# Transposed copies of x and memory from the host, one weight chunk for both token halves in the first block, and products on zeros during the first loads

## The chip, the cores and the metric

The kernel runs on 1 core of one Trainium2 chip. The metric is the device time of one execution in microseconds (us). Before the change it is 1037.3 us, the median of 3 runs (1035.68, 1037.3 and 1037.99 us).

The engines are named as in the profile: PE is TensorE (PEld its weight loads, which overlap with the products), ACT is ScalarE, DVE is VectorE, POOL is GpSimd, and SP is SyncE, whose queue issues all DMAs of this kernel.

## The reference

Two decoder layers work on 256 tokens of width 1024, beside 256 tokens of memory. Cut to what matters here:

```python
def rms_norm(x, gain):
    xf = x.astype(jnp.float32)
    y = xf * lax.rsqrt(jnp.mean(xf * xf, axis=-1, keepdims=True) + RMS_EPS)
    return (y * gain.astype(jnp.float32)).astype(x.dtype)

def swiglu(h, w_gate, w_up, w_down):
    return (jax.nn.silu(h @ w_gate) * (h @ w_up)) @ w_down

def memory_cross_attention(q_mem, mem_n, w_mem_kv, q_gain, k_gain):
    ...
    kv = mem_n @ w_mem_kv
    k = rms_norm(kv[..., :MEM_WIDTH].reshape(B, M, MEM_HEADS, HEAD_DIM), k_gain)
    v = kv[..., MEM_WIDTH:].reshape(B, M, MEM_HEADS, HEAD_DIM)
    ...
```

Layer 0 is x + 1/2 swiglu(norm(x)), then an mLSTM mixer beside attention to the memory, then a second half swiglu. Then keys and values for layer 1 are projected once. Layer 1 has a half swiglu, a dilated attention beside attention to the memory, and a last half swiglu. The hidden width of the swiglu is 2816. Each layer has its own gain for the memory (mem_norm) and its own w_mem_kv.

## The kernel before, in words

**Tiling.** The 256 tokens are two halves of 128 (t = 0 and 1). x stays on the chip as two [128, 1024] float32 tiles. A product contracts over the partitions, so x is needed transposed: `norm` (line 617) and `transposed` (line 590) turn 128x128 pieces of x on PE with an identity (into PSUM tile `tps`), ACT writes them times the gain as float32r (`xh`), and DVE writes what float32r leaves over (`xl`). The factor 1/rms of a token is applied later, where a product leaves PSUM.

**Three products for one.** Each weight chunk is split in the same way: ACT copies it to float32r (`hi`), DVE takes the difference (`lo`), and `mm3` (line 555) multiplies xh by lo, xh by hi and xl by hi into one PSUM bank.

**The weight stream.** `_stream` (line 48) lists all weights in the order of use as units of up to [128, 1024]. `load_unit` (line 462) issues the DMA of a unit into one of 6 tiles `raw`; `emit_unit` (line 473) splits it into one of 8 places `hi`, `lo`. A tile `raw` is free for the next load once DVE has taken `lo`; a place is free once the products of both halves have read it. In the first block (256 gate and 256 up columns of layer 0) a unit is one chunk of 128 rows, [128, 512], so 8 units; later a unit of a swiglu holds two chunks, [128, 1024].

**Order of the work.** The program is written out in one order by Python code that keeps rough cost tables of the engines (class `_Model`, line 168): PE's main stream is fixed, and side chains (splits, norms, activations) are put in where the tables say they are ready. Every engine, and SP's queue, then works strictly in the order in which its instructions were emitted.

**The swiglu.** `ffn` (line 720) runs 11 blocks of 256 hidden columns. `gu` makes a block for one half of the tokens: 8 chunks, three products each, 24 in all, into `gups`. `hidden` follows: silu on ACT (`sil`), the product with the up half on DVE (`h`), two transposes on PE (`tph`), the split to `hh` and `hl`. `dn` multiplies by w_down into four accumulators `acc`. In the first block, `gu(0, 0)` goes through all 8 units for half 0, and `gu(0, 1)` goes through them again for half 1.

**The memory.** `memory_load` (line 669) loads `mem` as two [128, 1024] tiles `mt`, once for each layer, and for layer 0 computes 1/rms. `memory_unit` (line 680) turns each tile on PE in two groups of four transposes and splits it into a place of the stream's ring, as the left operand of the products with w_mem_kv (`memory_kv`, line 787, PSUM tile `mkvps`).

**The start.** `run` (line 1341) loads the two halves of x[0], the identity, the gains, 5 weight units and x[1] in an order of its own, and puts the norms of both halves beside the main stream.

Of the kernel before, what the change touches and what calls it, by code (L numbers as in the profile page):

```python
# [35 lines left out]
FIRST = 4  # L36
TAIL = 3
START = 0.0
# [9 lines left out]
def _stream():  # L48
    """The weights in the order in which they are used: (key, source, slices, width)."""
# [37 lines left out]
    def memory(layer):  # L87
        units.append((("memT", layer, 0), None, 0))
        units.append((("memT", layer, 1), None, 0))
        single(("mkv", layer), "w_mem_kv", layer, 0, 512, 2)  # L90
# [23 lines left out]
def _pack(units, w):  # L114
    """Lay the weights out as one flat array, unit after unit, [128, width] each."""
    parts = []
    for _, src, _ in units:
        if src is None:
            continue
# [22 lines left out]
def _consts():  # L142
    """Constants of the shapes alone: identity, triangle, ones, selectors, T5 buckets, masks."""
# [122 lines left out]
class _Engine:  # L266
    """An engine of the core whose instructions the model follows."""
# [57 lines left out]
class _Chain:  # L325
    """A chain of steps that is emitted beside the main stream, each when the one before is done."""
# [6 lines left out]
class _Kernel:  # L333
# [74 lines left out]
    def until(self, t):  # L408
        """run the chains that are ready before the main stream can go on at t"""
# [19 lines left out]
    def wait(self, *chains):  # L429
        """in a chain: until others are done"""  # L430
# [30 lines left out]

    def load_unit(self):
        i, self.loaded = self.loaded, self.loaded + 1
        _, src, width = self.units[i]
        if src is None:
            return
# [6 lines left out]
    def emit_unit(self):  # L473
        """the next unit's steps begin: hi, the weights in float32r, and lo, what that leaves"""
        i, self.next = self.next, self.next + 1
        key, src, width = self.units[i]
# [11 lines left out]
        if src is None:  # L488
            c = self.spawn(self.memory_unit(key[2], hi, lo))
        else:  # L490
            while self.loaded <= i:
                self.room()
                self.load_unit()
            c = self.spawn(steps(self.raw.pop(i)))
            self.running.append(c)
            self.step(c)
# [11 lines left out]
    def unit_ready(self):  # L508
        """when the split of the next unit can begin without delaying other work"""
# [3 lines left out]
        if self.units[i][1] is None:  # L513
            return 0.0
# [19 lines left out]
    def release(self, *key):  # L534
        i = self.index[key]
        self.used[i] += 1
        while self.freed < len(self.units) and \
                self.used[self.freed] == (2 if self.units[self.freed][1] else 1):
# [27 lines left out]

    def rpow(self, ss, n, scale):
        """(ss * scale + eps) ** -0.5, [128, n]"""
# [7 lines left out]
    def rms(self, src, out, later=LATER):  # L576
        """out [128, 1] = 1 / rms of each row of src [128, 1024]"""
# [12 lines left out]
    def transposed(self, src, hi, lo, chunks, gain=None):  # L590
        """hi, lo [128, 8, 128] take the transposed 128-column chunks of src, times the gain"""
# [46 lines left out]
    def head_norm(self, src, n, out, rstd):  # L638
        """out = src * rstd normed over groups of 64; src [128, n*64] in PSUM"""
# [29 lines left out]
    def memory_load(self, layer):  # L669
        """the memory, ahead of its use"""  # L670
        self.mem_gain = self.gains[7 + layer]
        self.mem_tiles = []
        for m in range(2):
            mt = self.work.tile([P, D], F32, tag="mem", name="mt")
            self.nc.sync.dma_start(mt, self.io["mem"][0, m * P:(m + 1) * P, :])
            self.mem_tiles.append(mt)
            if layer == 0:
                self.mem_stats[m] = self.spawn(self.rms(mt, self.mem_rstd[m]))

    def memory_unit(self, m, hi, lo):  # L680
        mt = self.mem_tiles[m]
        yield from self.when(mt)
        h3, l3 = (a.rearrange("p (k t) -> p k t", k=NK) for a in (hi, lo))
        for h in range(2):
            yield from self.transposed(mt, h3, l3, [4 * h + j for j in range(4)], self.mem_gain)
            if h == 0:
                yield
# [16 lines left out]
    def block(self, x, key, n, kper, after):  # L704
        """a block of n columns of a projection; after(ps) are the steps that take it on"""
# [13 lines left out]

    def ffn(self, layer, which, after):  # L720
        nc = self.nc
        acc = [[self.acc.tile([P, 512], F32, tag="acc", name=f"acc{t}{h}") for h in range(2)]
               for t in range(2)]
        chains, hT = {}, {}
# [25 lines left out]
        def dn(b, t):  # L750
            self.finish(chains.pop((b, t)))
# [19 lines left out]
        for b in range(NB - 1):  # L771
            for t in range(2):
# [95 lines left out]
    def out_part(self, key, t, acc, haT, order, chunks, after=None):  # L868
        """some chunks of an output projection; the last ones end with the residual"""
# [21 lines left out]

    def mixer_a(self, after):
        nc, io = self.nc, self.io
        with ExitStack() as ctx:
# [44 lines left out]
            def gates():  # L939
                # u = i - cumsum(log sigmoid f), cg = max(0, running max of u)  # L940
# [165 lines left out]
            def first_block(t):  # L1106
                query_chains.append(self.block(t, ("a", "gq"), 264, 3, query(t)))
                if t == 1:
                    self.memory_load(0)
# [41 lines left out]

    def shared_kv(self, again):
# [49 lines left out]
        for b in range(3):  # L1202
            if b == 1:
                self.memory_load(1)
# [135 lines left out]

    def run(self, stop=None):
# [6 lines left out]
        nc.gpsimd.memset(self.mhalf, -0.5)  # L1348
# [102 lines left out]
```

## Time and profile before

| what | value |
|---|---|
| median of 3 runs | 1037.3 us (1035.68 to 1037.99) |
| span of the profiled execution | 1036.0 us |
| PE busy | 1019.0 us, 98% of the span, 4888 products and transposes |
| DVE busy | 616.1 us, 59% |
| ACT busy | 557.5 us, 54% |
| bytes moved by DMA | 182.53 MB, mean 176 GB/s |

The span runs from the first instruction to the last. Of the profiled execution the page gives the span alone, 1036.0 us; what lies around it is not told, and the 3 timed runs lie between 0.3 us below and 2.0 us above it.

To read it: the ends of products are modelled, so a product's own duration (0.39 us for 512 columns) is longer than its pitch, the time from the start of one to the start of the next (0.23 us). [...] A wait shows as a number in brackets behind a row: the idle time before it, and what ended it.

### The profile page before, as it was taken

What the parts mean: (1) busy time and instruction counts of PE and PEld (TensorE: products, weight loads), DVE (VectorE), ACT (ScalarE), POOL (GpSimd) and SP (SyncE); (2) the same over time, 40 slices, a digit from 0 to 9 for tenths busy, and PEclk for the clock granted to TensorE, in tenths of its full rate; (3) what the DMA queues carried; (4) which work ended last, traced back from release to release, by engine and by line L of the source; (5) the groups of instructions that cost most, each with busy time, mean ns of one, the idle gap of its engine ahead of it and who ended that gap; (6) DMA issues with size and microseconds to landing.
All of it is one profiled execution on the core that took longest, in us unless ns stands there. A gap on an engine that the chain in (4) does not pass through costs nothing.

```text
span 1036.0 us, 13199 instructions
## 1 busy us (share of the span) xinstructions
PE 1019.0 (98%) x4888; PEld 840.4 (81%) x4888; DVE 616.1 (59%) x903; ACT 557.5 (54%) x913; POOL 43.7 (4%) x78
## 2 busy tenths in 40 slices
PE   7999999999999999999999999999999999999998
PEld 5888888898888888888877888888887688888886
DVE  6655554767866755554565755455476865545452
ACT  7544453596775744454466644445366774545441
POOL 0000000111110000000011000000003000000000
PEclk9999999999999999999999999999999999999999
DMA  8764644553537465656454656464552246555531
GB/s 292 246 212 166 214 166 152 169 196 103 185 104 241 146 215 169 209 166 211 164 188 163 208 199 207 167 214 166 181 198 68 82 167 218 170 198 184 182 121 41
DMA packets 54329, 182.53 MB, mean 176 GB/s; under 512 B 6332, under 2 KB 8180, under 8 KB 54264
## 3 DMA queue, kind: packets, MB, share of 16 engines
q1 hardware_dynamic: 54264, 181.69, 52.0%
q8 instruction: 38, 0.62, 0.2%
q14 instruction: 27, 0.22, 0.1%
HBM read 180.60 MB, written 1.07 MB: 175 GB/s over the span
## 4 chain that ended last, share of the span: by engine, by line
PE 92%; DVE 3%; ACT 2%; DMA 1%; issue 1%; POOL 0%; SPq 0%; DVEq 0%; ACTq 0%
PE gups L545 47%; PE acc L545 23%; PE aps L545 6%; PE oacc L545 3%; PE bqps L545 2%; PE mkvps L545 2%; PE kvps L545 2%; PE tph L552 2%; PE tps L552 2%; DVE lo L276 1%; DMA raw<-in_wts 1%; PE sc L545 1%; DVE s L276 1%; PE ms L545 1%; PE po L545 0%
## 5 line engine op out<-in xcount | busy, mean ns | idle before, releaser
L276 DVE TENSOR_TENSOR lo<-raw,hi 128x1024 fp32r<-128x1024 f32 (+3 forms) x347 | 404.1, 1184 | 152.0 <-ACT hi L276 137.2
L276 ACT CAST hi<-raw 128x1024 fp32r<-128x1024 f32 (+3 forms) x347 | 349.3, 1021 | 110.7 <-PE acc L545 66.0
L545 PE MATMUL gups<-lo,xh 128*128 128x512 f32 x704 | 280.9, 399 | 1.3 <-DVE lo L276 1.3
L545 PE MATMUL gups<-hi,xl 128*128 128x512 f32 x704 | 275.8, 392 | 0.0
L545 PE MATMUL gups<-hi,xh 128*128 128x512 f32 x704 | 275.1, 391 | 0.0
L545 PEld LDWEIGHTS gups<-hi,xl 128*128 128x128 f32 x704 | 132.6, 188 | 28.5
L545 PEld LDWEIGHTS gups<-lo,xh 128*128 128x128 f32 x704 | 132.6, 188 | 28.5 <-DVE lo L276 2.9
L545 PEld LDWEIGHTS gups<-hi,xh 128*128 128x128 f32 x704 | 133.0, 189 | 25.9
L545 PE MATMUL acc<-lo,hh 128*128 128x512 f32 x352 | 141.8, 403 | 0.0
L545 PE MATMUL acc<-hi,hl 128*128 128x512 f32 x352 | 138.0, 392 | 0.0
L276 ACT ACTIVATE sil<-gups,rstd 128x256 f32<-128x256 f32 x88 | 41.8, 475 | 178.3 <-PE gups L545 178.3
L545 PE MATMUL acc<-hi,hh 128*128 128x512 f32 x352 | 137.2, 390 | 0.0
L276 DVE SCALAR_TENSOR_TENSOR h<-gups,rstd,sil 128x256 f32<-128x256 f32 x88 | 42.3, 481 | 140.9 <-ACT sil L276 140.9
L545 PEld LDWEIGHTS acc<-hi,hl 128*128 128x128 f32 x352 | 66.1, 188 | 14.5
L545 PEld LDWEIGHTS acc<-hi,hh 128*128 128x128 f32 x352 | 66.4, 189 | 12.6
L276 ACT CAST hh<-tph 128x256 fp32r<-128x256 f32 x88 | 32.8, 372 | 80.9 <-PE tph L552 80.9
L545 PEld LDWEIGHTS acc<-lo,hh 128*128 128x128 f32 x352 | 66.2, 188 | 12.2
L276 DVE TENSOR_TENSOR hl<-tph,hh 128x256 fp32r<-128x256 f32 x88 | 37.4, 425 | 39.7 <-ACT hh L276 39.7
L545 PE MATMUL aps<-lo,xh 128*128 128x384 f32 (+1 forms) x144 | 49.8, 346 | 0.0
L545 PE MATMUL aps<-hi,xl 128*128 128x384 f32 (+1 forms) x144 | 47.6, 330 | 0.0
L545 PE MATMUL aps<-hi,xh 128*128 128x384 f32 (+1 forms) x144 | 47.5, 330 | 0.0
L276 ACT ACTIVATE xh<-tps,gains 128x128 fp32r<-128x128 f32 x112 | 31.9, 373 | 24.8 <-PE tps L552 24.8
(176 smaller groups left out, 932.8 us busy)
## 6 DMA issues: line engine op xcount, KB each, us to landing
raw<-in_wts SPq DMA_DIRECT2D x304, 512.0 KB, 4.6
raw<-in_wts SPq DMA_DIRECT2D x32, 384.0 KB, 3.6
raw<-in_wts SPq DMA_DIRECT2D x8, 256.0 KB, 4.6
mt<-in_mem SPq DMA_DIRECT2D x4, 512.0 KB, 5.8
bias<-diag SPq DMA_DIRECT2D x1, 1536.0 KB, 8.0
x<-in_x SPq DMA_DIRECT2D x4, 256.0 KB, 3.6
out<-x SPq DMA_DIRECT2D x4, 256.0 KB, 2.0
raw<-in_wts SPq DMA_DIRECT2D x2, 396.0 KB, 3.5
```

What stands on the lines that cost most here:

```text
L276: call(out, *args, **kw)
L545: self.pe.matmul(out, lhsT=lhsT, rhs=rhs, start=start, stop=stop)
L552: self.pe.transpose(out, in_, ident)
```

## The change

Five edits.

1. The host lays out x transposed as well, in four pieces of [128, 2 chunks, 256 tokens] (`xT`), and the memory transposed (`memT`, two pieces of [128, 1024]). x itself is still loaded, for 1/rms and for the residual.
2. The memory's transposed pieces become units of the weight stream, two for each layer. `scaled` splits them with the gain: ACT and DVE read the loaded tile and not PSUM, and PE turns nothing. `mem` itself is loaded once, for 1/rms.
3. The first block is written out by `opening`: for each chunk k, ACT makes xh for both halves from `xraw`, DVE makes xl, and PE does six products, three for each half, into two PSUM banks, before it takes the next chunk. The accumulators `acc` get their banks after that.
4. At the start PE does 8 products of zeros (bf16, 512 columns) into an unused bank.
5. The first loads come in another order: pieces of xT between the first six weight units, then x in two loads of 512 KB, the constants, and the weight units from number 6 on.

```diff
@@ class _Kernel, emit_unit
         def steps(raw):
-            self.nc.scalar.copy(hi[:, :width], raw[:, :width])
-            yield
-            self.nc.vector.tensor_tensor(lo[:, :width], raw[:, :width],
-                                         hi.bitcast(F32)[:, :width], ALU.subtract)
+            if key[0] == "memT":
+                yield from self.scaled(*(a.rearrange("p (k t) -> p k t", k=NK) for a in (hi, lo, raw)),
+                                       self.gains[7 + key[1]])
+            else:
+                self.nc.scalar.copy(hi[:, :width], raw[:, :width])
+                yield
+                self.nc.vector.tensor_tensor(lo[:, :width], raw[:, :width],
+                                             hi.bitcast(F32)[:, :width], ALU.subtract)
...
+    def scaled(self, hi, lo, src, gain):
+
+        for h in range(2):
+            for k in range(4 * h, 4 * h + 4):
+                self.nc.scalar.activation(hi[:, k, :], src[:, k, :], AF.Copy, scale=gain[:, k:k + 1])
+            yield
+            for k in range(4 * h, 4 * h + 4):
+                self.nc.vector.scalar_tensor_tensor(lo[:, k, :], src[:, k, :], gain[:, k:k + 1],
+                                                    hi[:, k, :].bitcast(F32), ALU.mult, ALU.subtract)
...
-    def memory_unit(self, m, hi, lo):
-        mt = self.mem_tiles[m]
-        yield from self.when(mt)
-        h3, l3 = (a.rearrange("p (k t) -> p k t", k=NK) for a in (hi, lo))
-        for h in range(2):
-            yield from self.transposed(mt, h3, l3, [4 * h + j for j in range(4)], self.mem_gain)
...
+    def opening(self, ps, key):
+
+        nc = self.nc
+        self.xT = [self.xt_tiles(t) for t in range(2)]
+        gain = self.gains[0]
+        for k in range(NK):
+            x = self.xraw[k // 4][:, k % 4, :]
+            g = gain[:, k:k + 1]
+            parts = [[a[:, k, :] for a in self.xT[t]] for t in range(2)]
+            for t, (hi, _) in enumerate(parts):
+                nc.scalar.activation(hi, x[:, t * P:(t + 1) * P], AF.Copy, scale=g)
+            wh, wl = self.get(*key, k)
+            wh, wl = wh[:, :512], wl[:, :512]
+            for t, (hi, lo) in enumerate(parts):
+                nc.vector.scalar_tensor_tensor(lo, x[:, t * P:(t + 1) * P], g, hi.bitcast(F32),
+                                               ALU.mult, ALU.subtract)
+            for t, (hi, lo) in enumerate(parts):
+                self.matmul(ps[t], hi, wh, k == 0, False)
+            for t, (hi, lo) in enumerate(parts):
+                self.matmul(ps[t], hi, wl, False, False)
+            for t, (hi, lo) in enumerate(parts):
+                self.matmul(ps[t], lo, wh, False, k == NK - 1)
...
@@ ffn
         for b in range(NB - 1):
+            if (layer, which, b) == (0, 1, 0):
+                ps = [self.acc.tile([P, 512], F32, tag="acc", name="gups") for _ in range(2)]
+                self.opening(ps, ("gu", 0, 1, 0))
+                for t in range(2):
+                    chains[0, t] = self.spawn(hidden(0, t)(ps[t]))
+                continue
...
@@ run
+        warm = self.const.tile([P, 512], BF16, name="warm")
+        nc.vector.memset(warm, 0.0)
+        ps = self.tp.tile([P, 512], F32, tag="tp", name="warm")
+        for _ in range(WARM):
+            self.pe.matmul(ps, lhsT=warm[:, :P], rhs=warm, start=True, stop=True)
...
+        load_xT(0)
+        self.load_unit()
+        nc.sync.dma_start(g, io["gains"])
+        self.load_unit()
...
+        load_xT(1)
+        self.load_unit()
+        self.load_unit()
+        load_xT(2)
+        self.load_unit()
+        self.load_unit()
+        load_xT(3)
...
         for t in range(2):
-            for h in range(2):
-                first(t, h)
+            load_x(t)
+        nc.sync.dma_start(c, io["consts"][:, 0:3 * P])
```

On SP's queue at the start of the program the loads stood like this before (x0 and x1 are the two halves, raw0 to raw9 the weight units):

```order
L276 DMA x0_92<-in_x 128x512
L276 DMA consts_94<-in_consts 128x128
L276 DMA gains_96<-in_gains 128x78
L276 DMA raw0_98<-in_wts 128x512
L276 DMA x0_92<-in_x 128x512
L276 DMA raw1_101<-in_wts 128x512
L276 DMA raw2_103<-in_wts 128x512
L276 DMA raw3_105<-in_wts 128x512
L276 DMA raw4_107<-in_wts 128x512
L276 DMA x1_109<-in_x 128x512 x2
L276 DMA raw5_114<-in_wts 128x512
```

All of x and five of the eight units of the first block stand ahead of raw5. Now they stand like this from the seventh load on (ahead of these are the first two pieces of xT, raw0, the gains, raw1 and raw2):

```order
L273 DMA raw3_115<-in_wts 128x512
L273 DMA xraw_103<-in_xT 128x512
L273 DMA raw4_118<-in_wts 128x512
L273 DMA raw5_120<-in_wts 128x512
L273 DMA xraw_103<-in_xT 128x512
L273 DMA x0_124<-in_x 128x1024
L273 DMA x1_127<-in_x 128x1024
L273 DMA consts_123<-in_consts 128x384
L273 DMA sel_131<-in_consts 4x512
L273 DMA raw6_145<-in_wts 128x512
L273 DMA raw7_165<-in_wts 128x512
L273 DMA raw8_168<-in_wts 128x1024
```

Ahead of raw6 the queue now moves 1 MB of xT and 1 MB of x where it moved 1 MB of x, and raw5 stands ahead of x.

On ACT the last part of the first block is now this (xh0 and xh1 are the two halves of a chunk; the first pair here is chunk 6, the last is chunk 7; hi7 is the block's last weight unit, and hi8 to hi10 belong to the second block):

```order
L273 CAST hi7_250<-raw7_165 128x512
L273 ACTIVATE xh0_135<-xraw_103,gains_101 128x128
L273 ACTIVATE xh1_137<-xraw_103,gains_101 128x128
L273 CAST hi8_271<-raw8_168 128x1024
L273 CAST hi9_274<-raw9_171 128x1024
L273 ACTIVATE xh0_135<-xraw_103,gains_101 128x128
L273 ACTIVATE xh1_137<-xraw_103,gains_101 128x128
L273 CAST hi10_293<-raw10_190 128x1024
L273 ACTIVATE sil_300<-gups_133,rstd_126 128x256
L273 ACTIVATE sil_302<-gups_134,rstd_129 128x256
```

The x pieces of the last chunk stand behind the splits of units 8 and 9 of the next block.

On PE, where the memory of layer 1 was turned (second block of the shared keys and values, half 1), the order before was:

```order
L545 MATMUL kvps<-hi_4804,xl_4818 128x512
L552 MATMUL tps<-consts,mt 128x128 x4
L545 MATMUL kvps<-lo_4844,xh_4817 128x512
L545 MATMUL kvps<-hi_4843,xh_4817 128x512
L545 MATMUL kvps<-hi_4843,xl_4818 128x512
L552 MATMUL tps<-consts,mt 128x128 x4
```

Now the same place reads:

```order
L539 MATMUL kvps<-hi_4782,xl_4796 128x512
L539 MATMUL kvps<-lo_4822,xh_4795 128x512
L539 MATMUL kvps<-hi_4821,xh_4795 128x512
L539 MATMUL kvps<-hi_4821,xl_4796 128x512
L539 MATMUL kvps<-lo_4822,xh_4795 128x512
```

The four transposes of a group are gone, and the products close up; this holds for all eight groups of the two layers.

## Rows read from the trace of the kernel before

**Rows 1.** Part 1 of the page: busy time, share of the span and instructions of TensorE.
```profile
PE 1019.0 (98%) x4888; PEld 840.4 (81%) x4888; DVE 616.1 (59%) x903; ACT 557.5 (54%) x913; POOL 43.7 (4%) x78
```

**Rows 2.** Part 4 of the page: the chain of work that ended last, its shares of the span by engine.
```profile
PE 92%; DVE 3%; ACT 2%; DMA 1%; issue 1%; POOL 0%; SPq 0%; DVEq 0%; ACTq 0%
```

**Rows 3.** The timeline of TensorE from the start to the first product of the swiglu's second projection: start, us, operation, and in brackets the idle time before it and what ended it.
```profile
3.90 1.09 PE L552 MATMUL tps<-consts,x 128*128 128x128 f32 x4 [3.90 <-DMA consts<-in_consts]
...
7.97 0.80 PE L545 MATMUL gups<-lo,xh 128*128 128x512 f32 x1 [0.54 <-DVE lo L276]
...
8.56 0.63 PE L545 MATMUL gups<-hi,xh 128*128 128x512 f32 x1
...
8.99 0.63 PE L545 MATMUL gups<-hi,xl 128*128 128x512 f32 x1
...
10.42 0.80 PE L545 MATMUL gups<-lo,xh 128*128 128x512 f32 x1 [0.80 <-DVE lo L276]
...
14.60 0.40 PE L545 MATMUL gups<-hi,xh 128*128 128x512 f32 x1
...
18.11 0.39 PE L545 MATMUL gups<-lo,xh 128*128 128x512 f32 x1
...
23.81 0.39 PE L545 MATMUL gups<-lo,xh 128*128 128x512 f32 x1
...
35.24 0.39 PE L545 MATMUL acc<-lo,hh 128*128 128x512 f32 x1
```

**Rows 4.** The first load on SP's queue in the timeline; the same load in the view of DMA issues (KB, us from issue to landing); and two stretches of two microseconds (start:end, length, busy time of each engine, granted clock, share of the DMA engines, GB/s).
```profile
0.79 0.39 SPq L276 DMA_DIRECT2D x<-in_x  x1
...
x<-in_x SPq DMA_DIRECT2D x1, 256.0 KB, 2.8
...
14.00:16.00 2.00, 2.00 (x13) 1.69 (x12) 1.27 (x5) 2.00 (x7) 0.50 (x2) 1.00 0.82 299
16.00:18.00 2.00, 2.00 (x9) 1.35 (x8) 1.73 (x5) 1.39 (x5) 0.38 (x1) 1.00 1.00 393
```

**Rows 5.** The timeline of ScalarE and VectorE in the first 27 us; like instructions in a row are merged, with their count.
```profile
7.46 1.14 ACT L276 ACTIVATE xh<-tps,gains 128x128 fp32r<-128x128 f32 x4 [0.80 <-PE tps L552]
...
9.51 0.65 ACT L276 ACTIVATE junk<-x 128x512 bf16<-128x512 f32 x1
...
10.74 1.66 ACT L276 CAST hi<-raw 128x512 fp32r<-128x512 f32 x3
...
18.37 0.47 ACT L276 ACTIVATE sil<-gups,rstd 128x256 f32<-128x256 f32 x1 [0.98 <-PE gups L545]
...
20.21 2.00 ACT L276 CAST hi<-raw 128x1024 fp32r<-128x1024 f32 x2
...
8.64 1.13 DVE L276 SCALAR_TENSOR_TENSOR xl<-tps,gains,xh 128x128 fp32r<-128x128 f32 x4 [0.72 <-ACT xh L276]
...
18.87 0.48 DVE L276 SCALAR_TENSOR_TENSOR h<-gups,rstd,sil 128x256 f32<-128x256 f32 x1 [0.33 <-ACT sil L276]
...
21.56 4.62 DVE L276 TENSOR_TENSOR lo<-raw,hi 128x1024 fp32r<-128x1024 f32 x4
```

**Rows 6.** Groups of ScalarE's instructions in the first 30 us, different shapes apart: count, busy us, mean ns of one, idle time before.
```profile
L276 ACT CAST hi<-raw 128x1024 fp32r<-128x1024 f32 x8 | 8.0, 1048 | 0.2 <-PE gups L545 0.2
L276 ACT CAST hi<-raw 128x512 fp32r<-128x512 f32 x8 | 4.6, 634 | 0.0
L276 ACT ACTIVATE xh<-tps,gains 128x128 fp32r<-128x128 f32 x16 | 4.6, 373 | 4.1 <-PE tps L552 4.1
```

**Rows 7.** The transposes of the memory on TensorE: the group over the whole span (count, busy us, mean ns, idle before), and one of the eight groups of four in the timeline.
```profile
L552 PE MATMUL tps<-consts,mt 128*128 128x128 f32 x32 | 4.8, 274 | 0.0
...
227.30 0.34 PE L545 MATMUL aps<-hi,xl 128*128 128x384 f32 x1
227.47 0.60 PE L552 MATMUL tps<-consts,mt 128*128 128x128 f32 x4
227.83 0.42 PE L545 MATMUL aps<-lo,xh 128*128 128x384 f32 x1
228.09 0.34 PE L545 MATMUL aps<-hi,xh 128*128 128x384 f32 x1
```

**Rows 8.** Two stretches, with the memory's transposes in layer 0 and in layer 1: start:end, length, busy us (and instructions) of PE, PEld, DVE, ACT and POOL, granted clock, share of the DMA engines, GB/s.
```profile
222.00:236.00 14.00, 14.00 (x89) 13.63 (x87) 11.16 (x24) 13.37 (x28) 0.00 (x0) 1.00 0.56 187
...
550.00:562.00 12.00, 11.58 (x62) 9.44 (x63) 7.14 (x21) 8.68 (x24) 1.26 (x3) 1.00 0.28 103
```

**Rows 9.** The timeline of TensorE at the shared keys and values, around the product `pb` of the relative bias.
```profile
531.75 0.39 PE L545 MATMUL kvps<-hi,xl 128*128 128x512 f32 x1
534.62 0.80 PE L545 MATMUL pb<-hot,rel 32*12 32x384 f32 x2 [2.49 <-DMA raw<-in_wts]
...
536.22 0.63 PE L545 MATMUL kvps<-lo,xh 128*128 128x512 f32 x1
...
539.57 0.39 PE L545 MATMUL kvps<-hi,xl 128*128 128x512 f32 x1
```

**Rows 10.** The issue of the two loads of the memory for layer 0 on SP's queue, ScalarE's split of the first two units of w_mem_kv, and the first product that uses the memory.
```profile
210.72 0.90 SPq L276 DMA_DIRECT2D mt<-in_mem  x2
...
226.92 1.99 ACT L276 CAST hi<-raw 128x1024 fp32r<-128x1024 f32 x2
...
236.95 0.50 PE L545 MATMUL mkvps<-lo,hi 128*128 128x512 f32 x1
```

More of the change, by code (lines that the diff above doesn't have):

```diff
@@ L35 @@
 EARLY = 0.0
-FIRST = 4
+WARM = 8
 TAIL = 3
-START = 0.0
 A_ORDER = (6, 7, 0, 1, 2, 3, 4, 5)
@@ L87, in memory @@
     def memory(layer):
-        units.append((("memT", layer, 0), None, 0))
-        units.append((("memT", layer, 1), None, 0))
+        for m in range(2):
+            units.append((("memT", layer, m), ("memT", None, None, m, 1), D))
         single(("mkv", layer), "w_mem_kv", layer, 0, 512, 2)
@@ L463, in load_unit @@
         i, self.loaded = self.loaded, self.loaded + 1
-        _, src, width = self.units[i]
-        if src is None:
-            return
+        width = self.units[i][2]
         raw = self.rawp.tile([P, 1024], F32, tag="raw", name=f"raw{i}")
@@ L475, in emit_unit @@
         i, self.next = self.next, self.next + 1
-        key, src, width = self.units[i]
+        key, _, width = self.units[i]
         hi = self.ring.tile([P, 1024], F32R, tag="hi", name=f"hi{i}")
@@ L537, in release @@
         while self.freed < len(self.units) and \
-                self.used[self.freed] == (2 if self.units[self.freed][1] else 1):
+                self.used[self.freed] == (1 if self.units[self.freed][0][0] == "memT" else 2):
             self.tiles.pop(self.freed)
@@ L667, in query_rms, with memory_stats @@
         nc.gpsimd.tensor_tensor(out, ss[:, :n], self.mhalf[:, :n], ALU.pow)
-    def memory_load(self, layer):
-        self.mem_gain = self.gains[7 + layer]
-        self.mem_tiles = []
+    def memory_stats(self):
         for m in range(2):
@@ L716, in block @@
         return self.holder[b]
+    def opening(self, ps, key):
[20 more added lines that the diff above has]
+            for t in range(2):
+                self.release(*key, k)
+            self.tick()
     def ffn(self, layer, which, after):
         nc = self.nc
-        acc = [[self.acc.tile([P, 512], F32, tag="acc", name=f"acc{t}{h}") for h in range(2)]
-               for t in range(2)]
-        chains, hT = {}, {}
+        acc, chains, hT = [], {}, {}
         def hidden(b, t):
@@ L750, in dn @@
         def dn(b, t):
+            if not acc:
+                self.finish(chains[0, 0], chains[0, 1])
+                acc.extend([self.acc.tile([P, 512], F32, tag="acc", name=f"acc{t}{h}")
+                            for h in range(2)] for t in range(2))
             self.finish(chains.pop((b, t)))
@@ L771, in ffn @@
         for b in range(NB - 1):
+            if (layer, which, b) == (0, 1, 0):
+                ps = [self.acc.tile([P, 512], F32, tag="acc", name="gups") for _ in range(2)]
+                self.opening(ps, ("gu", 0, 1, 0))
+                for t in range(2):
+                    chains[0, t] = self.spawn(hidden(0, t)(ps[t]))
+                continue
             for t in range(2):
@@ L1348, in run @@
         nc.gpsimd.memset(self.mhalf, -0.5)
+        warm = self.const.tile([P, 512], BF16, name="warm")
[3 more added lines that the diff above has]
+            self.pe.matmul(ps, lhsT=warm[:, :P], rhs=warm, start=True, stop=True)
+        g = self.const.tile([P, 78], F32, name="gains")
+        self.gains = [g[:, i * NK:(i + 1) * NK] for i in range(9)]
+        heads = [g[:, 72 + i:73 + i] for i in range(6)]
@@ new lines, in run, with load_xT, load_x @@
+        self.mk, self.mq, self.kg, self.qg = heads[0:2], heads[2:4], heads[4], heads[5]
+        self.xraw = [self.work.tile([P, 4, 2 * P], F32, tag="mem", name="xraw") for _ in range(2)]
+        def load_xT(q):
+            nc.sync.dma_start(self.xraw[q // 2][:, 2 * (q % 2):2 * (q % 2) + 2, :], io["xT"][q])
+        def load_x(t):
+            self.x.append(self.keep.tile([P, D], F32, name=f"x{t}"))
+            nc.sync.dma_start(self.x[t], io["x"][0, t * P:(t + 1) * P, :])
+            self.rstd[t] = self.keep.tile([P, 1], F32, tag=f"rstd{t}", bufs=2, name="rstd")
+            self.stats[t] = self.spawn(self.rms(self.x[t], self.rstd[t], LATER))
@@ L1359, in run @@
+        self.load_unit()
+        self.load_unit()
+        load_xT(2)
+        self.load_unit()
+        self.load_unit()
+        load_xT(3)
         c = self.const.tile([P, 384], F32, name="consts")
-        nc.sync.dma_start(c[:, 0:P], io["consts"][:, 0:P])
         self.ident, self.tri, self.ones = (c[:, i * P:(i + 1) * P] for i in range(3))
-        g = self.const.tile([P, 78], F32, name="gains")
-        nc.sync.dma_start(g, io["gains"])
-        self.gains = [g[:, i * NK:(i + 1) * NK] for i in range(9)]
@@ L1365, in run @@
-        g = [g[:, 72 + i:73 + i] for i in range(6)]
-        self.mk, self.mq, self.kg, self.qg = g[0:2], g[2:4], g[4], g[5]
-        self.load_unit()
-        load_x(0, 1)
-        for _ in range(FIRST):
-            self.load_unit()
-        for h in range(2):
-            load_x(1, h)
-        first = self.then(0, later=START)
         for t in range(2):
-            for h in range(2):
-                first(t, h)
+            load_x(t)
+        nc.sync.dma_start(c, io["consts"][:, 0:3 * P])
@@ L1378, in store @@
+        self.sel = self.const.tile([4, 512], F32, name="sel")
+        nc.sync.dma_start(self.sel, io["consts"][0:4, 384:896])
         def store(t, h):
@@ L1382, in run @@
         then = self.then
-        self.loads()
-        nc.sync.dma_start(c[:, P:], io["consts"][:, P:3 * P])
-        self.sel = self.const.tile([4, 512], F32, name="sel")
-        nc.sync.dma_start(self.sel, io["consts"][0:4, 384:896])
         self.ffn(0, 1, store if stop == 1 else then(1))
```

36 lines of the change are left out of this document (9 added, 27 removed).

## The prediction

> **What bounds the kernel now.** I read the engines' shares first: TensorE is busy 98% of the span and VectorE, the next, 59% [rows 1]. Then the chain that ended last: 92% of it is TensorE [rows 2]. So almost anywhere a microsecond of work taken from PE is a microsecond of time, and work on the other engines or on the queue is free as long as PE doesn't wait for it. The exception is the start, so I read PE's timeline there. PE has nothing to do until 3.90 us, when the first transposes run. Its first product starts at 7.97, and the second chunk's at 10.42 after a wait for a split. [...] At 18.11 half 1 of the first block begins, at 23.81 the second block, at 35.24 its successor; from 18.11 to 23.81 are 24 products and two transposes, so a product of 512 columns takes 0.23 [rows 3]. Up to 35.24 PE does 96 products of 0.23, 22 us; 13 us of that stretch is start, waits, slow clock and transposes. That is what the change can reach at the start, together with the memory's transposes later on.
>
> **The transposes of the memory go.** There are 32, in eight groups of four. A group holds PE from 227.47 to 227.83, 0.36, and the product behind it has 0.26 where its neighbours have 0.17 (227.30 to 227.47), so a group costs 0.45 and eight cost 3.6 us [rows 7]. They lie where PE has no idle time in layer 0 and 0.4 us in 12 in layer 1 [rows 8], so all of it should be gained. What replaces them: ACT and DVE split the same pieces, 8 and 8 instructions for each tile as before, from the loaded tile and not from PSUM. In layer 0 VectorE has 11.16 busy of 14 us there, but ScalarE 13.37 [rows 8]; it works ahead, though: the first units of w_mem_kv were split at 226.92 and used at 236.95 [rows 10], so a PE that comes 1.8 us sooner still finds them. I cost it at nothing; if ScalarE's lead were used up, layer 0's half of the gain, 1.8, would go.
>
> In layer 0 two more loads of 512 KB stand on SP's queue behind `mt`. The loads of `mt` were issued at 210.72, and the first product on the memory starts at 236.95, 26 us later [rows 10]; the DMA engines are 56% busy on the way [rows 8]. 1 MB at 393 GB/s [rows 4] takes 2.7 us, a tenth of the lead. Cost nothing; if the lead were gone, 2.7 us.
>
> [...] ACT's cast from a loaded tile takes 1048 ns at 1024 columns and 634 at 512, so 0.81 ns for a column and 0.32 us for 128 columns; the same width from PSUM took 0.373 [rows 6]. [...]
>
> **The start, step by step.** The first products now need no transposes, but they stand behind loads and behind ScalarE's order. ScalarE makes the x pieces of chunk 7 only after it has split units 8 and 9 of the next block, so the first block can't end before unit 9 has landed. Ahead of and with unit 9 the queue moves 1.05 MB of xT, 2.10 MB of units 0 to 7, 1.05 MB of x, 0.24 MB of small loads and 1.05 MB of units 8 and 9, 5.49 MB. The first 0.26 MB lands at 0.79 + 2.8 = 3.6. The rate is 393 GB/s in a stretch with a full queue and 299 in one where it had to wait for tiles [rows 4]. I take 360, nearer the full one: 5.23 MB in 14.5 us, so unit 9 lands at 18.1. At 393 it is 16.9, at 299 21.1.
>
> From there [rows 5]: the split of unit 9 on ACT, 1.00 (2.00 for two), to 19.1; the two x pieces at 1.14/4, to 19.7; their remainders on DVE at 1.13/4, to 20.3; the last two of the six products behind them, to 20.9. The second block then begins at 20.9 where it began at 23.81.
>
> In the second block ACT splits unit 10 to 20.7, makes both `sil` (0.47 each) to 21.9 and splits unit 11 (landed at 21.0) to 22.9. DVE takes `lo` of units 9 and 10 (4.62/4 = 1.15 each) to 22.6, both `h` to 23.6, and unit 11 to 24.7. PE does unit 8 and half of unit 9 to 22.9, waits until 23.6 for the second `h`, turns both (0.25), and goes through the rest of unit 9 to 24.5, unit 10 to 25.9 and unit 11 to 27.3, 15 products of 0.23. Half 1 with one pair of transposes is 5.7: the third part of the program begins at 33.0 where it began at 35.24. So the start gives 2.2 us; 3.2 at 393 GB/s, where ScalarE's own work takes over (16 pieces of 0.285, 8 splits of 0.55, 2 x 1.23 for the squares `junk` from 9.51 to 10.74, two splits of 1.0: 13.5 us from about 5.0), and a loss of 0.8 at 299.
>
> **Products on zeros.** Eight of 0.43 at most are 3.4 us, from about 1 to 4.5, where PE had nothing to do before 3.90. They cost nothing. What they bring I also put at nothing: chunk 1 waits for ScalarE behind units 2 and 3, which at 360 GB/s land at 7.3, so a fast chunk 0 only waits longer.
>
> **Clock in the opening.** Between chunks PE waits again, so the clock may be low at chunk 7. The nearest row: after the wait of 2.49 us for `pb` eight products ran 0.42 apart, from 536.22 to 539.57, 1.5 us more than at 0.23 [rows 9]. So this term is 0 to 1.5 us or somewhat more; I take 0, since chunks 2 to 5 have their data in a row and are worked off without a break.
>
> **What stays.** The wait for `pb` and the slow products behind it: the loads and products around it keep their order, and I leave them. If the wait went, 2.5 and 1.5 would go; if it grew, no row bounds it but itself.
>
> **Sum.** -3.6 - 2.2 = -5.8. Against the profiled span of 1036.0 that is 1030.2; the median of the runs lies 1.3 above the span, so 1031.5.
>
> **Rivals.**
> - The clock stays low through the waiting chunks. For it: before, products with waits between them ran at 0.43 until 3.9 us of unbroken work had passed (10.42 to 14.3 [rows 3]). Against: the opening has such a stretch in chunks 2 to 5. If chunk 7 starts low, 3.9 us at half pace lose 1.9: 1033.4. [...]
> - The start gives nothing: the loads come at about 300 GB/s, or ScalarE's order holds chunk 7 longer than I count. Then only the transposes count, less up to 0.8: 1033.7 to 1034.5. For it: 1 MB more goes ahead of unit 6.
> - The wait for `pb` or its slow clock happens to go: up to 4.0 more, about 1028. Nothing in the order speaks for it.
> - Slower: the loads fall behind. Unit 11 sets the end of the second block, 12 us before the third part begins. To be 2.1 us slower in all, the third part must begin at 35.24 + 3.6 + 2.1 = 40.9, unit 11 land at 28.9, and 6.27 MB come in 25.3 us: below 248 GB/s. The price is 1 us for each microsecond that unit 11 is later than 21.0. No stretch of full queue is that slow. Time then: 1039.5 or more.
> - That the change doesn't do what it says: the order of instructions shows that it does.
>
> **How the numbers follow.** Forecast 0.50, clock 0.19, start gives nothing 0.17, `pb` 0.08, slower 0.06. Less than 0.2% (2.1 us) is no change to this measurement: faster is below 1035.2, slower above 1039.4. The first, the second and the fourth case and most of the third are faster; I give 0.82 to faster, 0.12 to same, 0.06 to slower. The range of 8 in 10 goes from 1028.5 (full rate at the start, and part of `pb`) to 1036.0 (299 GB/s and a slow clock: 1037.3 - 3.6 + 0.8 + 1.5).
>
> **What would show it.** Right: no transposes of `mt`; unit 9 lands near 18; the x pieces of chunk 7 on ScalarE right behind its split; the second block's first product near 21 and the third part's near 33; the pitch 0.23 from chunk 3 on; the wait before `pb` unchanged. Wrong: a pitch of 0.43 beyond chunk 7; a first product of the third part later than 35; new waits of PE in the mixer of layer 0 for memory or weights; any loss or gain behind 35 us other than the eight groups.

## The result, and the profile after

The changed kernel takes 1040.6 us (median of five runs, 1038.7 to 1043.6) against 1036.8 for the kernel before on the same chip (five runs, 1035.7 to 1038.0): a ratio of 1.0033, interval 1.0017 to 1.005. By the ratio it is slower by 3.4 us; 1031.5 was forecast.

TensorE's share and the chain look as in [rows 1, 2] (PE is still 98% busy), so the place has to be found by going through PE's timeline from its start and comparing it with that of before.

```profile
PE 1019.6 (98%) x4848; PEld 836.6 (81%) x4848; DVE 616.2 (59%) x904; ACT 561.9 (54%) x915; POOL 44.2 (4%) x78
...
PE 90%; DVE 3%; ACT 3%; DMA 1%; issue 1%; POOL 1%; SPq 0%; DVEq 0%; ACTq 0%
```

TensorE's timeline of the changed kernel (start, us, operation, idle time before and what ended it), from the start, from the projections of the memory in layer 0, and from `pb`:

```profile
6.61 1.22 PE L539 MATMUL gups<-hi,xh 128*128 128x512 f32 x2 [1.77 <-ACT hi L273]
...
19.87 0.79 PE L539 MATMUL gups<-hi,xh 128*128 128x512 f32 x2 [0.77 <-ACT xh L273]
...
21.42 0.39 PE L539 MATMUL gups<-lo,xh 128*128 128x512 f32 x1
...
33.09 0.39 PE L539 MATMUL acc<-lo,hh 128*128 128x512 f32 x1
...
233.16 0.50 PE L539 MATMUL mkvps<-lo,hi 128*128 128x512 f32 x1
...
237.94 0.40 PE L539 MATMUL mkvps<-hi,lo 128*128 128x512 f32 x1
241.42 0.49 PE L539 MATMUL mkvps<-lo,hi 128*128 128x512 f32 x1 [3.09 <-DVE lo L273]
...
242.32 6.76 PE L539 MATMUL sc<-qT,kT 128*128 128x256 f32 x16
248.87 4.01 PE L539 MATMUL pn<-vx,w 128*128 128x193 f32 x12
...
537.90 0.80 PE L539 MATMUL pb<-hot,rel 32*12 32x384 f32 x2 [0.79 <-DMA mask<-in_consts]
```

Against [rows 3] the second block begins 2.4 us sooner (21.42 for 23.81) and the next part 2.15 sooner (33.09 for 35.24). Against [rows 10] the first product on the memory is 3.8 us sooner (233.16 for 236.95). So far all is as forecast. Then PE waits 3.09 us for `lo` of the fourth unit of w_mem_kv, a wait that before doesn't have, and behind it the sixteen products `sc` take 6.76 us. `sc` are the products of queries and keys (`qT`, `kT`) of the mixer's first heads, `pn` those of their weights with the values; `y` is the convolution from which `kT` is made, `e` are exponentials of the gates, and `tpc` the transposes that `y` is read from. In before `sc` stands behind the projections:

```profile
250.81 3.73 PE L545 MATMUL sc<-qT,kT 128*128 128x256 f32 x16
```

The stretches say why they are slow (start:end, length, busy us of PE, PEld, DVE, ACT, POOL, granted clock, share of the DMA engines, GB/s): the granted clock is 0.53 of full from 242 to 253, and 1.00 ahead of that and behind it.

```profile
236.00:242.00 6.00, 2.65 (x12) 1.68 (x10) 4.50 (x9) 5.49 (x7) 1.04 (x4) 1.00 0.35 119
242.00:253.00 11.00, 11.00 (x32) 7.59 (x31) 4.23 (x10) 2.30 (x6) 0.00 (x0) 0.53 0.34 109
253.00:260.00 7.00, 6.47 (x31) 5.09 (x29) 4.29 (x12) 2.48 (x9) 3.62 (x6) 1.00 0.20 56
```

The wait is for VectorE, but VectorE had waited for ScalarE. ScalarE's timeline, here of the changed kernel:

```profile
17.53 1.98 ACT L273 CAST hi<-raw 128x1024 fp32r<-128x1024 f32 x2
19.42 0.69 ACT L273 ACTIVATE xh<-xraw,gains 128x128 fp32r<-128x128 f32 x2
...
232.88 1.04 ACT L273 CAST hi<-raw 128x1024 fp32r<-128x1024 f32 x1
...
236.45 0.47 ACT L273 ACTIVATE y<-tpc,convw 128x256 f32<-128x256 f32 x1 [2.05 <-PE tpc L546]
236.94 1.28 ACT L273 ACT_TABLE_LOAD   x1
238.24 0.94 ACT L273 ACTIVATE e<-e 128x384 f32<-128x384 f32 x2
239.08 1.03 ACT L273 CAST hi<-raw 128x1024 fp32r<-128x1024 f32 x1
240.12 1.28 ACT L273 ACT_TABLE_LOAD   x1
241.42 0.85 ACT L273 ACTIVATE kT<-y 128x768 f32<-128x768 f32 x1
```

And the same place in before:

```profile
233.44 2.04 ACT L276 CAST hi<-raw 128x1024 fp32r<-128x1024 f32 x2
235.33 0.53 ACT L276 ACTIVATE y<-tpc,convw 128x256 f32<-128x256 f32 x1
...
240.23 0.47 ACT L276 ACTIVATE y<-tpc,convw 128x256 f32<-128x256 f32 x1 [2.14 <-PE tpc L552]
...
244.57 0.47 ACT L276 ACTIVATE y<-tpc,convw 128x256 f32<-128x256 f32 x1
...
248.40 0.85 ACT L276 ACTIVATE kT<-y 128x768 f32<-128x768 f32 x1
```

Before, the third and fourth unit are split together, well ahead of the last `y` (244.57), and `kT` is done at 249.25, 1.6 us before `sc` asks for it. After, the fourth stands behind the last `y` (236.45), a table load and two `e`, and `y` itself waits for PE's transposes `tpc`. ScalarE idles 2.05 us in front of a split that could have been made (an experiment below makes it at 234.75). `kT`, which `sc` needs, stands yet behind it. No line of the diff asks for this: the planner chose another order. What tipped it wasn't tested. Its own clocks of the engines stand otherwise without the transposes, and the diff also takes away the rule by which the memory's units were always ready (`unit_ready`); two of the planner's numbers undo it (below).

### The profile page after: what moved, and what is told of

Read it like the earlier page. It is cut to its first block, busy times and chain, and to the rows that moved or that the text cites. A ratio compares the mean times of both kernels' runs of the same rounds, so it can differ in the third digit from the quotient of the medians.

```text
span 1036.9 us, 13132 instructions
## 1 busy us (share of the span) xinstructions
PE 1019.6 (98%) x4848; PEld 836.6 (81%) x4848; DVE 616.2 (59%) x904; ACT 561.9 (54%) x915; POOL 44.2 (4%) x78
## 4 chain that ended last, share of the span: by engine, by line
PE 90%; DVE 3%; ACT 3%; DMA 1%; issue 1%; POOL 1%; SPq 0%; DVEq 0%; ACTq 0%
PE gups L539 46%; PE acc L539 22%; PE aps L539 7%; PE oacc L539 3%; PE bqps L539 2%; PE tph L546 2%; PE mkvps L539 2%; DVE lo L273 1%; PE kvps L539 1%; ACT hi L273 1%; PE tps L546 1%; PE sc L539 1%; POOL rp_r L273 1%; DVE s L273 1%; PE ms L539 1%
## 5 line engine op out<-in xcount | busy, mean ns | idle before, releaser
L273 ACT ACTIVATE xh<-tps,gains 128x128 fp32r<-128x128 f32 x96 | 27.2, 375 | 20.9 <-PE tps L546 20.9
```

The costliest lines, as they stand in the source:

```text
L273: call(out, *args, **kw)
```

## The experiments

**One split early.** The first theory: PE waits because that one split is queued behind work that itself waits for PE, and the slow clock follows from the wait.

```
             vproj(0)
+            self.get("mkv", 0, 6)
             self.finish(*query_chains)
```

> The changed kernel, with one line more: the split of the fourth unit of w_mem_kv of layer 0 is taken right after the projection of the values, so it stands on ScalarE ahead of y, the table load and the two e; with it the planner leaves sc and pn of the first heads behind the projections of the memory. Theory 1 (PE waits 3.1 us for that split because it was queued behind work that itself waits for PE, and the halved clock behind it costs some 5 more): no wait of PE over 0.5 us in the projections of the memory, no stretch at the half clock from 242 on, and the whole gain of 5.8 that was predicted less what a later place gives back, 1031 to 1033 us against 1036.8 for the kernel before. Theory 2 (the order of sc and pn alone lowers the clock): the same time here, since both are gone. Theory 3 (the unit itself, its load, comes too late for the earlier PE): the wait of 3 us stays, the time stays at about 1040.

Measured: 1032.4 us, ratio 0.9955 (0.9938 to 0.9972), a gain where the changed kernel had a loss. The wait and the slow clock are gone, and `sc` runs at full clock (granted 1.00 from 242 to 253):

```profile
244.97 3.74 PE L539 MATMUL sc<-qT,kT 128*128 128x256 f32 x16
248.54 2.13 PE L539 MATMUL pn<-vx,w 128*128 128x193 f32 x12
```

Against these rows the changed kernel has 3.09 of waiting, 3.0 more in `sc` and 1.9 more in `pn`: 8.0 us; the medians differ by 8.2. That is the whole loss. (The two traces differ by 4.9 only: in that of the early split the next part begins 0.5 later, at 33.59, and the first block of shared keys, with `pb`, takes 2.5 more, 16.62 for 14.08.) Its place is settled, its cause not, since this line moved both the split and `sc`.

**The two parts apart.** The kernel before with the hunks of the start alone, and with those of the memory alone.

> The kernel before with the new start alone (x transposed from the host, the first block for both halves of the tokens, products on zeros); the memory is loaded and turned on PE as before. Theory 1: the second block begins 2.4 us sooner, the first product of the down projection 2.2 sooner, and that reaches the end: 1034.6 us against 1036.8, no wait of 3 us and no stretch at half clock in the mixer of layer 0. [...]

> The kernel before with the memory from the host alone; the start is that of before. On ScalarE the fourth unit of w_mem_kv stands behind y, the table load and the two e, as in the changed kernel, and sc and pn stand inside the projections of the memory. Theory 1: 1.6 us gained until the first product of the memory, then a wait of about 3 us and some 5 us of half clock; slower than the changed kernel by the 2.2 us of the start: 1042 to 1043 us against 1036.8. Rival (the stall needs the sooner start as well): 1033 to 1034 us.

Measured: 1035.0 us for the start, ratio 0.9981 (0.9967 to 0.9995), and 1042.5 for the memory, ratio 1.0054 (1.0039 to 1.007). The start gives 1.9 of the 2.2 forecast. In its trace the next part begins only 1.3 sooner (33.96 for 35.24), and PE waits 1.10 at `pb` for 2.49 before [rows 9], so part of the 1.9 may be `pb`'s. The memory alone brings the stall, with the start of before, so a sooner start isn't needed for it:

```profile
243.94 0.79 PE L540 MATMUL mkvps<-lo,hi 128*128 128x512 f32 x1 [3.14 <-DVE lo L274]
...
245.39 6.68 PE L540 MATMUL sc<-qT,kT 128*128 128x256 f32 x16
```

**The split early, PE's order kept.** This tells the split from the place of `sc`. The early split as above, and between the fourth unit's products the planner is let run on, so that it puts `sc` and `pn` there again:

```
                          k + j == 0, k + j == NK - 1)
+                if key == ("mkv", 0) and k + j == 6:
+                    self.until(self.now + 6.0)
```

> The changed kernel with the split of the fourth unit of w_mem_kv ahead of y and e on ScalarE, but with PE's order kept as in the changed kernel: sc and pn of the first heads stay between the fourth unit's products. Theory 1 (wait first, clock after it): no wait for lo, sc's sixteen products in some 3.7 us as in the kernel before instead of 6.76, 1031 to 1034 us. Theory 2 (sc and pn in that place cost the time, by themselves or by a wait of their own for kT): PE waits at sc instead, 2 us or more, and the clock falls; 1037 to 1040 us.

Measured: 1041.9 us, ratio 1.0045 (1.0029 to 1.0061), as slow as the changed kernel. The first theory falls as it stands: taking this wait away wins nothing by itself. The wait for `lo` is gone, and another of much the same size has its place. TensorE and ScalarE there:

```profile
244.03 5.98 PE L539 MATMUL sc<-qT,kT 128*128 128x256 f32 x16 [3.74 <-ACT kT L273]
```

```profile
241.84 1.28 ACT L273 ACT_TABLE_LOAD   x1 [0.22 <-DVE y L273]
243.13 0.84 ACT L273 ACTIVATE kT<-y 128x768 f32<-128x768 f32 x1
```

`sc` was placed ahead of the time at which `kT` can be there. In the changed kernel two waits lie over each other, for `lo` until 241.42 and for `kT` until some 242.3, and a reader of the trace sees only the first. With `sc` in that place it hardly matters where the split stands (1041.9 for 1040.6).

**The heads behind the memory.** So the place of `sc` is changed, by exchanging two lines:

```
-            chains = heads(0, waits)
             mem = self.memory_kv(0, mp)
+            chains = heads(0, waits)
```

> The changed kernel with two lines exchanged: the chains of the first heads are begun behind the projections of the memory instead of ahead of them, so sc and pn can't be put inside these. The split of the fourth unit stands ahead of y and kT on ScalarE again. Theory 2 (the place of sc on PE, ahead of the time at which kT can be there, costs 3 to 4 us of waiting and then the clock): no wait over 0.5 us in the projections of the memory, full clock in sc and pn, 1032 us, give or take 1, as in the run with the early split and sc behind. If the heads, begun later, hold up what follows: 1035 or more.

Measured: 1032.3 us, ratio 0.9961 (0.995 to 0.9972). The largest wait in the projections is 0.8, a little over what was expected, and the time is that of the early split. But `sc` isn't all that moved: as was expected, the planner now splits the fourth unit ahead of `y`, with the two behind it, and so this run has both moves, like the early split:

```profile
234.65 2.51 ACT L273 CAST hi<-raw 128x1024 fp32r<-128x1024 f32 x3
```

**A wait without `sc` behind it.** Does the idle time lower the clock, or do the narrow products of `sc`? And what does the late split cost with `sc` out of the way? The two lines exchanged, and in `unit_ready` the split of that unit held back until PE asks for it:

```
-        if i >= min(len(self.units), self.freed + RING):
+        if i >= min(len(self.units), self.freed + RING) or self.units[i][0] == ("mkv", 0, 6):
             return 1e9
```

> The exchange of the two lines again, and the split of the fourth unit of w_mem_kv is held back until PE's order asks for it, so that it stands on ScalarE behind y and kT; sc and pn stand behind the projections of the memory. PE waits for the split as in the changed kernel, 2 to 5 us, but what stands behind the wait is products of 512 columns. If the idle time alone lowers the clock: a stretch at half clock of 3.4 us or more from within 2 us of the wait's end, and the time is over the run without the wait by the wait and half of that stretch, 1036 to 1039. If the fall needs sc's narrow products behind the wait: full clock right behind it, over the run without the wait by the wait alone, 1034 to 1036.

Measured: 1037.9 us, 5.6 over the run without the wait (1032.3). TensorE there:

```profile
242.04 0.79 PE L539 MATMUL mkvps<-lo,hi 128*128 128x512 f32 x1 [3.14 <-DVE lo L273]
242.63 0.63 PE L539 MATMUL mkvps<-hi,hi 128*128 128x512 f32 x1
...
247.75 0.60 PE L539 MATMUL mkvps<-hi,hi 128*128 128x512 f32 x1
248.18 0.41 PE L539 MATMUL mkvps<-hi,lo 128*128 128x512 f32 x1
248.43 0.39 PE L539 MATMUL mkvps<-lo,hi 128*128 128x512 f32 x1
```

From 242.63 to 247.75 the products of 512 columns stand 0.43 apart though none waits (granted clock 0.53 from 241 to 248), and 0.23 after that (0.99 from 248 to 255). So here the clock fell behind 3.14 us of idle time with no narrow products behind it: 3.1 of waiting, and fourteen products that each lose 0.2, 2.8. With `sc` and `pn` behind the wait the slow stretch is longer in the changed kernel (11 us at 0.53), but not in the run above with a wait for `kT`, where the clock was back by 252 (0.51 from 245 to 252, 1.00 from 252 to 259); what makes the difference stays open.

These runs tell the two causes apart. The late split alone costs 5.6 (1037.9 against 1032.3), `sc` ahead of `kT` alone 9.5 (1041.9 against 1032.4), and both together, in the changed kernel, 8.2. So each is enough for most of the loss, they don't add up, and the loss goes only when both are mended.

**Without the products on zeros.** `WARM = 0`.

> The changed kernel without the eight products on zeros. Theory A (the start is set by the loads and by ScalarE's share of them): the second block begins within 0.5 us of where the four runs with the new start had it, 21.4 to 22.8, and the time is that of the changed kernel, 1040.6, within 1 us. Theory B (the products on zeros bring the full clock sooner, and that is worth time): the clock rises later than the 9.5 to 13.6 us seen with them, the second block begins at 23.5 or later, 1041.5 us or more.

Measured: 1040.8 us, ratio 1.004 (1.0024 to 1.0056), the changed kernel's time. The second block begins inside the span of the other runs, and from the second chunk on a pair of products takes 0.80 us and less, where the first took 1.22:

```profile
6.81 1.22 PE L539 MATMUL gups<-hi,xh 128*128 128x512 f32 x2 [6.81 <-ACT hi L273]
...
10.29 0.80 PE L539 MATMUL gups<-hi,xh 128*128 128x512 f32 x2 [0.55 <-ACT xh L273]
10.93 0.62 PE L539 MATMUL gups<-lo,xh 128*128 128x512 f32 x2
...
22.54 0.39 PE L539 MATMUL gups<-lo,xh 128*128 128x512 f32 x1
```

They neither cost nor bring anything that can be measured.

**The planner's numbers.** `unit_ready` lets a split go at once if fewer than AHEAD units are split and unused, and else only if ScalarE and VectorE have less than SLACK of work before it. One number each.

> The changed kernel with one number of the planner changed, AHEAD from 3 to 6: up to six units are split as soon as they are there, whatever ScalarE and VectorE have to do. The planner then puts the split of the fourth unit of w_mem_kv ahead of y and sc and pn behind the projections of the memory by itself. If the lost time is the planner's choice in this one place: no wait over 1 us there, 1031 to 1034 us. If splits taken so early hold up the chains of the mixers elsewhere: 1036 or more, with waits of PE for ScalarE or VectorE in other places.

> The changed kernel with another number of the planner changed, SLACK from 0.8 to 1.2: a split may be put on ScalarE while it has up to 1.2 us of work before it. The same order comes out in the mixer of layer 0: the split early, sc and pn behind the projections. If the lost time is the planner's choice in this one place: 1031 to 1034 us; otherwise 1036 or more.

Measured: AHEAD 6 gives 1035.3 us, ratio 0.9977 (0.9966 to 0.9989), SLACK 1.2 gives 1033.9, ratio 0.9969 (0.9957 to 0.998). Both planners split the fourth unit early, leave `sc` behind the projections, and lose the stall. AHEAD 6 came between what was expected: the stall is gone, but in the mixer of layer 1 PE now has two waits that no other run has at this length, and behind the longer one a granted clock of 0.50 from 809 to 812, after 1.00 from 800 to 808 (what PE waited for: us in total, times, longest).

```profile
PE tpp L546 <- DVE s L273: 2.2, 1, 2.2
...
PE tpp L546 <- ACT pTb L273: 1.7, 1, 1.7
```

**`pb` later.** In the early-split run PE waited 1.76 us for the loads of the biases at `pb`, and the products behind it stood 0.43 apart from 533.10 to 535.24, and 0.23 after that. Here `pb` is put later in that kernel:

```
             nc.sync.dma_start(mask, io["consts"][0:12, 1280:1664])
-            yield
+            yield 6.0
```

> The kernel with the early split, and pb, the product on the table of the biases in the shared keys' stage, put 6 us later in the planner's time, so that its loads (hot, mask) have landed. In the run with the early split alone PE waited 1.8 us at pb and then had the half clock for 3.4 us, which costs 1.7. If both go and nothing follows: 1029 us (1032.4 less 3.5). If the wait for kn at tpk behind it, 2.4 us in two places, grows instead: 1031 to 1032.5.

Measured: 1030.5 us, ratio 0.9939 (0.9924 to 0.9953); PE has no wait at `pb` any more, and the products behind it stand 0.23 apart (from 537.90 on).

```profile
536.82 0.81 PE L539 MATMUL pb<-hot,rel 32*12 32x384 f32 x2
```

The gain of 2.0 lies between the two cases. The traces differ there by 3.7, where 3.5 was expected, so the other runs of the early split probably waited less at `pb`; in the profiles of this study that wait is 0.6 to 2.5 us long, 1.1 and 2.5 in two kernels with the same order there.

**ScalarE's order at the start.** In that kernel the pieces of x of chunks 6 and 7 are made ahead of the splits of units 6 to 9, those of 2 and 3 right after the split of unit 1, and the planner isn't asked for other work before chunk 5:

```
             wh, wl = self.get(*key, k)
+            if k in (1, 3, 5):
+                turn(k + 1, k + 2)
...
-            self.tick()
+            if k > 4:
+                self.tick()
```

> The kernel with the early split and the later pb, and ScalarE's work in the first block put in the order in which the loads land: the pieces of x of two chunks, then the splits of two weight chunks, with nothing else between before chunk 5. In all runs with the new start PE waited 0.3 to 1.3 us for xh of an early chunk and 0.8 for xh of chunk 7, which stands on ScalarE behind the splits of the next block's first two units. If that order holds the first block up: these waits go, the second block begins 1 to 2 us sooner (at 20 to 21.5 instead of 22.5), 1029 us against 1030.5. If the loads and the half clock of the first products set it, or the next block's first units now come as much later: no change, 1030 to 1031.

Measured: 1029.0 us, ratio 0.9923 (0.9909 to 0.9937), the fastest. PE has no wait for `xh` any more, and the second block begins 2.5 us sooner than in the run with `pb` alone moved (22.48), of which the next part keeps 1.6:

```profile
20.01 0.50 PE L539 MATMUL gups<-lo,xh 128*128 128x512 f32 x1
```

So the change's idea holds: with the split early and `sc` later it beats the kernel before by 4.5 us, and with the two further moves by some 8.

## Why the prediction was wrong

- **The step that failed** is the sentence on what replaces the transposes: that ScalarE works ahead, "so a PE that comes 1.8 us sooner still finds them", costed at nothing, with 1.8 as the price if its lead were used up. The lead was read from the first two units [rows 10]; the fourth had none, since the planner set its split behind work that waits for PE. New waits of PE in this mixer stood among the prediction's signs of being wrong, but in none of its chances. And it was taken for granted that only PE's time would change, not the order. The new order puts `sc` among the projections, 3 to 4 us before `kT` is there. The price is not 1.8 but 8.0: 3.1 of waiting and 4.9 of slow clock, and it has two causes, the late split and the early `sc`. The rival on the slower side named the loads; no wait in this mixer was for a load.
- **The transposes**, 3.6 forecast: right as work of PE, not all of it as time. In layer 0 PE gains 1.6 from the 49th product of the mixer's projections (207.10 before, 204.87 after) to the first product on the memory (29.85 before, 28.29 after). In layer 1 the second block of shared keys takes 14.54 before and 13.09 after, 1.45. Each stretch of the changed kernel also holds a pair of other transposes that stood outside it before (the first two rows below), worth 0.2 and 0.3; without these the gain is 3.5. But in layer 1 most of it is lost again in the next half block, where PE waits for `kn`, which it didn't before; over the second block and that half it gains 0.3 (20.96 before, 20.63 after):

```profile
231.27 0.38 PE L546 MATMUL tpc<-consts,pre 128*128 128x128 f32 x2
...
556.78 0.41 PE L546 MATMUL tpk<-consts,kn 128*128 128x128 f32 x2
...
564.63 0.44 PE L546 MATMUL tpk<-consts,kn 128*128 128x128 f32 x2 [1.27 <-DVE kn L273]
```

  And the last row's place in before:

```profile
564.04 0.41 PE L552 MATMUL tpk<-consts,kn 128*128 128x128 f32 x2
```

  In times, start and memory with the early split (1032.4) against the start alone (1035.0) give 2.6; the start alone has 0.8 of that wait. "All of it should be gained" failed there too.
- **The start**, 2.2 forecast, gives 1.9 alone. Unit 9 landed at 17.9 and the next part began at 33.09, as worked out (18.1, 33.0); in the other runs with this start it began 0.4 to 1.3 later, so the agreement is in part luck; and the second block began 0.5 later than worked out (21.42 for 20.9) and took that much less. ScalarE's order did hold chunk 7: its pieces of x follow the splits of units 8 and 9 directly (17.53, 19.42), and PE waits 0.77.
- **Reading the tiles instead of PSUM**: the sixteen pieces of the memory in layer 0 took ScalarE 4.9 us, 0.31 each, where sixteen from PSUM took 4.6, 0.29 [rows 6]. They are not cheaper by 0.05, as the prediction's figures have it (0.32 for 0.373, the 0.32 an estimate from casts of 1024 and 512 columns): by the mean of one they are dearer by 0.03 (404 ns for 373).
- **The products on zeros** at nothing: right. **The clock in the opening** at nothing: right by the pitch from chunk 3 on (pairs of products of 0.61 to 0.63 us in chunks 3 to 5), and chunk 7's pairs took 0.79, 0.63 and 0.62 after its wait of 0.77.
- **`pb` unchanged**: not so. Its wait was 0.8 instead of 2.5, without a slow clock (granted 1.00 from 531.25 to 545.33; before, 0.51 from 536.0 to 539.5): the first block of shared keys, with `pb`, took 17.40 before and 14.08 after (both halves, 526.28 to 543.68 and 531.25 to 545.33), so 3.3 us came back here in this trace. It changes from run to run and belongs into the range, not into the sum.

## What to carry to other kernels

Where a planner sets the order, a removed instruction moves others that it never touched: compare the order on PE and on the engine that feeds it over the whole stage, and ask of each product that moved forward when its last input can be there. A wait that the trace names may lie over a second one; take each away in an experiment, alone and with the other, before one is called the cause. A stall in a stream of products is to be costed with the slow clock behind it, where the clock falls: here 0.6 times the wait (at `pb` before [rows 9]) to 1.6 times (4.9 on 3.1).

## What the runs showed of the hardware

The clock was at half for a stretch after these idle times of PE: 2.49 us at `pb` in before (granted 0.51 from 536.0 to 539.5), 1.76 there with the split early (products of 512 columns 0.43 apart instead of 0.23, from 533.10 to 535.24), 2.21 at `tpp` with AHEAD 6 (0.50 from 809 to 812), and in the mixer of layer 0 3.09 in the changed kernel (0.53 from 242 to 253), 3.14 with the split held back and `sc` behind (0.53 from 241 to 248) and 3.74 with the split early and PE's order kept (0.51 from 245 to 252). PE had been busy before (6.00 of 6 us from 526 to 532 in before, 10.00 of 10 from 225 to 235 in the changed kernel), and the products behind ran without a gap (3.50 of 3.5 and 11.00 of 11 us in the slow stretches of these two).

No such stretch shows after waits at `pb` of 0.79 in the changed kernel (granted 1.00 from 531.25 to 545.33), of 0.6 with SLACK 1.2 (mean granted clock of the profiled execution 1.000) and of 1.1 with the start alone (0.999), after one of 1.7 at `tpp` with AHEAD 6 (its mean, 0.998, is accounted for by the one stretch above), and after one of 1.85 at `tpk` with the split early and PE's order kept (products of 512 columns 0.23 apart right behind it).

In the opening the granted clock reads 1.00 in before and in the changed kernel (from 8 to 10 us in both), though products of 512 columns stood 0.43 apart, so the slow part shows there in the pitch alone. Pairs of products that started 0.85 apart came to 0.45 to 0.48 at 10.1, 10.7, 13.2, 13.5 and 14.0 us in five kernels with the same products on zeros, and at 10.9 without them; with ScalarE's order at the start changed, the first two pairs stood 0.72 and 0.65 apart, those from 8.24 on 0.85, and those from 11.57 on 0.46. So there is no steady gain to be had from the products on zeros here.
